# Between the two passes of a down projection: later pairs' preparation also waits its turn on ScalarE, and two sums between banks move behind the fourth pair

## The chip, the cores and the metric

The kernel runs on one core of one Trainium2 chip. The metric is device time in microseconds (us) of one execution. Before the change the median of three runs is 743.40 us (743.13 to 743.85).

## What is computed

One layer of a decoder trunk over 512 positions of width 1024, in float32:

```
h = RMSNorm(x);  q, k, v, gates = h @ W_in
m = sigmoid(gate_a) * (moba_attention @ W_a) + sigmoid(gate_b) * (stick_breaking_attention @ W_b)
x = x + m @ W_out
h = RMSNorm(x)
u_gate, u_val = split(causal_conv(h @ w_up))        # each 512 x 2816
x = x + (silu(u_gate) * u_val) @ w_down             # w_down: 2816 x 1024
out = RMSNorm_final(x)
```

Only the last product, the down projection `(silu(u_gate) * u_val) @ w_down`, is touched by the change.

## The kernel before, in words

**Every float32 product is three matmuls.** A matrix is split into a rounded part `hi` and a rest `lo`; `mm3` (lines 71 to 74) issues hi·hi, hi·lo and lo·hi on TensorE. The split of a weight tile of 128x1024 is one copy on ScalarE (`whi`, line 594) and one subtraction on VectorE (`wlo`, line 595), in `split_w`; that of an activation tile is the same pair of operations in `split_out` (lines 261 to 263).

**The down projection in two passes.** The 22 blocks of 128 rows of `w_down` are taken as nine pairs of blocks and four single ones (18 to 21). The pairs are multiplied as 2x2 block products by a scheme with seven instead of eight products. Eight PSUM banks hold the result, two for each quarter: `c11`, `c21`, `c12`, `c22` (each with `t` 0 and 1).

- The **first pass** (lines 603 to 616) adds four products for each pair: into c22, c21, c11 and c12. For the ninth pair the order is c11, c12, c21, c22.
- The **hand-over** (lines 637 to 649) combines the banks: `p1s` is a copy of c11 on ScalarE, `u2` = c12 + p1s, c21 is raised by u2, c12 becomes c22 + u2, and c22 becomes c21 + p5s, where `p5s` is a copy of the old c22 on ScalarE. The sums are on VectorE.
- The **second pass** (lines 650 to 654) adds three products for each pair: into c11, c21 and c12, 18 matmuls of 128x512. It does not touch c22.
- After the seventh pair 32 transposes (lines 667 to 670) add the residual to all eight banks, `x1R`; then come pairs eight and nine, then the four single blocks, `wl` (line 673), and the final norm.

**Preparation of a pair for the second pass** is `prep` (lines 628 to 634): VectorE makes `t2` (line 629), ScalarE and VectorE split the raw weight tile (`whi`, `wlo`), the activations (`xs`, three blocks of 256) and t2 (`w4`). That is three operations on ScalarE and four on VectorE. Two pairs are prepared ahead of the loop (line 636); the loop's turn j prepares pair j+2.

**What sets the order.** TensorE's program is in the order in which it is written. On the other engines a planner places instructions by its own estimate of when their inputs are there; each engine then works through its list in that fixed order. `tc.issue_after(x)` keeps the planner from placing what is inside ahead of instruction x on the engine of x. Before the change the preparation in the loop stands inside `tc.issue_after(last.ins)`, where `last` is an instruction of VectorE: the last sum of the hand-over, then the last operation of the pair before. Nothing of the kind holds it on ScalarE.

**Buffers.** Raw weight tiles have five buffers (`wraw`), split tiles seven (three in `wsp`, four in `dsp`), `xs` and `w4` three each. Loads are issued by SyncE (`rload`, line 586) in program order; the loads of `x1R` (line 661) and of `gb` (line 663) stand between those of the seventh and the eighth pair.

Of the kernel before, what the change touches and what calls it, by code (L numbers as in the profile page):

```python
# [10 lines left out]
F32 = mybir.dt.float32  # L11
F32R = mybir.dt.float32r
BF = mybir.dt.bfloat16
AF = mybir.ActivationFunctionType
# [13 lines left out]
NP = 9  # L28
# [10 lines left out]
def trunk_layer(ctx: ExitStack, tc: tile.TileContext, xT: bass.AP, w: bass.AP, vec: bass.AP,  # L39
                gfin: bass.AP, trig: bass.AP, out: bass.AP):  # L40
    nc = tc.nc

    def pool(stack, name, bufs, space=None, side=None):
        kw = {}
        if space is not None:
            kw["space"] = space
        if side is not None:
            kw["side"] = side
        return stack.enter_context(tc.tile_pool(name=name, bufs=bufs, reuse_waits="tile", **kw))
# [21 lines left out]
    def mm3(ps, a, b, start, stop, **kw):  # L71
        nc.tensor.matmul(ps, a[0], b[0], start=start, stop=False, **kw)  # L72
        nc.tensor.matmul(ps, a[0], b[1], start=False, stop=False, **kw)  # L73
        nc.tensor.matmul(ps, a[1], b[0], start=False, stop=stop, **kw)  # L74

    def blk(t, k, n=128):
        return t[0][:, k * n:(k + 1) * n], t[1][:, k * n:(k + 1) * n]
# [181 lines left out]
                fillers.pop(0)  # L259

    def split_out(hl, o):
        nc.scalar.activation(hl[:, 0], o, AF.Copy)
        return nc.vector.tensor_sub(hl[:, 1], o, hl[:, 0].bitcast(F32))

    stk = {}

    def rotate(g, n, i, ps, half):
        sc = (0.125, 1.0)[n]
        half[i] = [rt.tile([128, S], F32, name=f"r{i}{j}") for j in range(2)]
        for j in range(2):  # L270
            nc.vector.scalar_tensor_tensor(half[i][j], ps, sc, tg[:, j], op0=OP.mult, op1=OP.mult)
        if i:
            out = []
            for j, op in ((0, nc.vector.tensor_sub), (1, nc.vector.tensor_add)):
                o = half[0][j]
                op(o, o, half[1][1 - j])
                hl = mqkp.tile([128, 2, S], F32R, name=f"hl{j}")
                split_out(hl, o)
                out.append(hl)
            stk.setdefault(("a", g), []).append(out)  # L280
# [7 lines left out]
    def sb_qk(p):  # L288
        sc = {}

        def use(n, nm, ps):
            o = hlp.tile([128, S], F32, name="o")
            if nm == "q":
                nc.vector.scalar_tensor_tensor(o, ps, 0.125, rb, op0=OP.mult, op1=OP.mult)
            else:
                nc.vector.tensor_mul(o, ps, rb)
            sc[nm] = mqkp.tile([128, 2, S], F32R, name=f"hl{n}")
            split_out(sc[nm], o)

        for n, nm in enumerate(("q", "k")):  # L300
            yield from proj(("sqk", p, n), lambda ps: use(n, nm, ps))
        stk["b", p] = [(sc["q"], sc["k"], h * 64) for h in range(2)]
# [176 lines left out]
    for i in range(KT):  # L479
        if i >= NG:  # L480
            fillers.append(gates(i))
            fill(1000)
        wab = wload(("ab", i))
        g = pend[i]
        for b, br in enumerate("ab"):
            ps = pmm.tile([128, S], F32, name="mm")
            for p in range(4):
                mm3(ps, blk(wab, b * 4 + p), (yhl[br, p][:, 0], yhl[br, p][:, 1]), p == 0, p == 3)
            nc.vector.tensor_mul(g[b], g[b], ps)
        nc.vector.tensor_add(g[0], g[0], g[1])  # L490
        split_out(mhl[i], g[0])
# [48 lines left out]
    for i in range(FT):  # L540
        uc = []
        for b in range(2):
# [4 lines left out]
            t = up.tile([128, S], F32, name=f"t{b}")  # L547
# [11 lines left out]
        j = i // 2  # L559
# [17 lines left out]
    cq = {n: [pd.tile([128, 512], F32, name=f"{n}{t}") for t in range(2)] for n in ("c11", "c21", "c12", "c22")}  # L577
# [6 lines left out]
    def rload(key):  # L584
        raw = wraw.tile([128, 1024], F32, name="raw")
        nc.sync.dma_start(raw, w[WIDX[key]])
        return raw

    def split_w(raw):
        p = wsp if nsplit[0] % 7 < 3 else dsp  # L590
        nsplit[0] += 1
        hi = p.tile([128, 1024], F32R, name="whi")
        lo = p.tile([128, 1024], F32R, name="wlo")
        nc.scalar.activation(hi, raw, AF.Copy)  # L594
        nc.vector.tensor_sub(lo, raw, hi.bitcast(F32))  # L595
        return hi, lo

    def prod(bank, a, b, wt, h, start, stop, **kw):
        for t in range(2):
            sl = slice(t * 128, (t + 1) * 128)  # L600
            mm3(bank[t], (a[:, 0, b, sl], a[:, 1, b, sl]), blk(wt, h, 512), start, stop, **kw)
# [18 lines left out]
    cmb = pool(ctx, "cmb", 1)  # L620
# [7 lines left out]
    def prep(j, ra):  # L628
        nc.vector.tensor_sub(t2[j], ra[:, :512], t2[j])
        wa = split_w(ra)  # L630
        xs = xsp.tile([128, 2, 3, 256], F32R, name="xs")
        w4 = xsp.tile([128, 2, 512], F32R, name="w4")
        split_out(xs.rearrange("p a b c -> p a (b c)"), xb[j].rearrange("p b c -> p (b c)"))
        return xs, wa, (w4[:, 0], w4[:, 1]), split_out(w4, t2[j])

    ready = [prep(j, rload(("down", 2 * j + 1))) for j in range(2)]
    for t in range(2):
        p1s = cmb.tile([128, 512], F32, name=f"p1s{t}")
        nc.scalar.activation(p1s, cq["c11"][t], AF.Copy)
        u2 = cmb.tile([128, 512], F32, name=f"u2{t}")  # L640
        nc.vector.tensor_add(u2, cq["c12"][t], p1s)
        cq["u2", t] = u2
    for t in range(2):
        nc.vector.tensor_add(cq["c21"][t], cq["c21"][t], cq["u2", t])
    for t in range(2):
        p5s = cmb.tile([128, 512], F32, name=f"p5s{t}")
        nc.scalar.activation(p5s, cq["c22"][t], AF.Copy)
        nc.vector.tensor_add(cq["c12"][t], cq["c22"][t], cq["u2", t])
        last = nc.vector.tensor_add(cq["c22"][t], cq["c21"][t], p5s)
    for j in range(NP):  # L650
        xs, wa, w4, _ = ready.pop(0)
        prod(cq["c11"], xs, 0, wa, 0, False, False, skip_group_check=True)
        prod(cq["c21"], xs, 2, w4, 0, False, False, skip_group_check=True)
        prod(cq["c12"], xs, 1, wa, 1, False, False, skip_group_check=True)
        if j + 2 < NP:
            ra = rload(("down", 2 * j + 5))
            with tc.issue_after(last.ins):
                ready.append(prep(j + 2, ra))
                last = ready[-1][3]
        if j < KT // 2:  # L660
            nc.sync.dma_start(x1R[j], x1D[j])
        if j == KT // 2:
            nc.sync.dma_start(gb, gfin[None, :].to_broadcast([128, D]))
        if j == NP - 3:
            for t in range(QT):
                for h in range(2):
                    for i in range(4):
                        nc.tensor.matmul(acc[t, h][:, i * 128:(i + 1) * 128],  # L668
                                         x1R[2 * h + i // 2][:, i % 2, t * 128:(t + 1) * 128], ident,
                                         is_transpose=True, start=False, stop=False, skip_group_check=True)  # L670
# [3 lines left out]
    for t in range(QT):  # L674
        o = on[:, t]
# [91 lines left out]
```

## Time and profile before

| | us |
|---|---|
| median of three runs | 743.40 |
| the profiled execution's own time | 744.41 |
| its span, first to last instruction | 742.7 |
| TensorE busy with matmuls | 726.1 |
| VectorE busy | 511.2 |
| ScalarE busy | 327.0 |
| mean granted TensorE clock | 0.991 of full speed |

The time is that of the whole execution, the span that of the instructions in it. Busy time is summed over all instructions of an engine. Matmuls are pipelined and overlap in the records: two start 0.23 us apart, and each is shown with 0.39. An idle stretch of an engine is put down to what released it.

### The profile page before, as it was taken

What the parts mean: (1) busy time and instruction counts of PE and PEld (TensorE: products, weight loads), DVE (VectorE), ACT (ScalarE), POOL (GpSimd) and SP (SyncE); (2) the same over time, 40 slices, a digit from 0 to 9 for tenths busy, and PEclk for the clock granted to TensorE, in tenths of its full rate; (3) what the DMA queues carried; (4) which work ended last, traced back from release to release, by engine and by line L of the source; (5) the groups of instructions that cost most, each with busy time, mean ns of one, the idle gap of its engine ahead of it and who ended that gap; (6) DMA issues with size and microseconds to landing.
All of it is one profiled execution on the core that took longest, in us unless ns stands there. A gap on an engine that the chain in (4) does not pass through costs nothing.

```text
span 742.7 us, 9689 instructions
## 1 busy us (share of the span) xinstructions
PE 726.1 (98%) x3836; PEld 602.5 (81%) x3836; DVE 511.2 (69%) x724; ACT 327.0 (44%) x468; POOL 21.6 (3%) x40
## 2 busy tenths in 40 slices
PE   9999999999999999999999999999999999978996
PEld 6888888879788888888888888888888888856885
DVE  7778776692964544445648877878787888759813
ACT  7344453563652332334435434344443445465413
POOL 0000000320310000000000000000000000000000
PEclk9999999999999999999999999999999999997998
DMA  8432211121224323224432232332323134583203
GB/s 312 175 101 71 79 37 57 44 76 53 87 86 171 113 85 101 99 88 153 143 112 100 86 113 86 101 98 86 113 86 111 63 111 150 192 312 118 79 1 113
DMA packets 25389, 80.95 MB, mean 109 GB/s; under 512 B 2816, under 2 KB 3456, under 8 KB 25344
## 3 DMA queue, kind: packets, MB, share of 16 engines
q1 hardware_dynamic: 23472, 77.06, 30.9%
q10 hardware_dynamic: 1872, 3.28, 1.2%
q8 instruction: 30, 0.49, 0.3%
q14 instruction: 15, 0.12, 0.1%
HBM read 76.13 MB, written 4.19 MB: 108 GB/s over the span
## 4 chain that ended last, share of the span: by engine, by line
PE 70%; issue 20%; DVE 6%; DMA 3%; ACT 1%; POOL 0%; DVEq 0%; ACTq 0%; POOLq 0%
PE mm L72 20%; PE mm L74 19%; PE mm L73 19%; PE c L72 3%; DMA raw<-w 3%; PE c L73 3%; PE c L74 3%; DVE wlo L595 2%; PE tp L415 1%; PE tp L397 1%; ACT whi L594 1%; PE sc L330 1%; DVE raw L607 1%; DVE R L368 1%; PE c L668 0%
## 5 line engine op out<-in xcount | busy, mean ns | idle before, releaser
L67 ACT ACTIVATE whi<-raw 128x1024 fp32r<-128x1024 f32 (+2 forms) x106 | 107.0, 1013 | 212.8 <-PE mm L73 131.0
L72 PE MATMUL mm<-h,whi 128*128 128x512 f32 x352 | 137.1, 390 | 0.0
L74 PE MATMUL mm<-h,wlo 128*128 128x512 f32 x352 | 137.0, 389 | 0.0
L73 PE MATMUL mm<-h,whi 128*128 128x512 f32 x352 | 136.9, 389 | 0.0
L68 DVE TENSOR_TENSOR wlo<-raw,whi 128x1024 fp32r<-128x1024 f32 (+2 forms) x106 | 122.6, 1162 | 16.5 <-ACT whi L67 16.1
L72 PE MATMUL mm<-xg,whi 128*128 128x512 f32 x224 | 89.9, 401 | 0.0
L74 PE MATMUL mm<-xg,wlo 128*128 128x512 f32 x224 | 87.4, 390 | 0.0
L73 PE MATMUL mm<-xg,whi 128*128 128x512 f32 x224 | 87.3, 390 | 0.0
L73 PEld LDWEIGHTS mm<-h,whi 128*128 128x128 f32 x352 | 66.1, 188 | 13.8
L72 PEld LDWEIGHTS mm<-h,whi 128*128 128x128 f32 x352 | 66.1, 188 | 13.7
L74 PEld LDWEIGHTS mm<-h,wlo 128*128 128x128 f32 x352 | 66.1, 188 | 13.6
L546 DVE TENSOR_TENSOR u<-mm,rb 128x512 f32<-128x512 f32 x44 | 30.3, 690 | 30.6 <-PE mm L74 30.4
L72 PEld LDWEIGHTS mm<-xg,whi 128*128 128x128 f32 x224 | 42.1, 188 | 9.8 <-issue 1.4
L74 PEld LDWEIGHTS mm<-xg,wlo 128*128 128x128 f32 x224 | 42.0, 188 | 9.1
L73 PEld LDWEIGHTS mm<-xg,whi 128*128 128x128 f32 x224 | 42.2, 188 | 7.8
L594 ACT ACTIVATE whi<-raw 128x1024 fp32r<-128x1024 f32 x31 | 32.3, 1053 | 28.9 <-DVE raw L607 14.0
L595 DVE TENSOR_TENSOR wlo<-raw,whi 128x1024 fp32r<-128x1024 f32 x31 | 37.5, 1219 | 3.2 <-ACT whi L594 3.2
L548 ACT ACTIVATE t<-u,vecs 128x512 f32<-128x512 f32 x44 | 35.2, 802 | 2.0 <-DVE u L546 2.0
L439 DVE TENSOR_TENSOR g<-mm,rb 128x512 f32<-128x512 f32 x16 | 11.0, 687 | 34.4 <-PE mm L74 34.4
L551 DVE SCALAR_TENSOR_TENSOR t<-u,vecs,t 128x510 f32<-128x510 f32 x44 | 32.9, 749 | 1.3
L549 DVE SCALAR_TENSOR_TENSOR t<-u,vecs,t 128x511 f32<-128x511 f32 x44 | 32.8, 745 | 1.3 <-ACT t L548 1.3
L554 ACT ACTIVATE t<-t 128x512 f32<-128x512 f32 x22 | 13.8, 628 | 35.5 <-DVE t L551 35.5
(202 smaller groups left out, 1275.1 us busy)
## 6 DMA issues: line engine op xcount, KB each, us to landing
raw<-w SPq DMA_DIRECT2D x127, 512.0 KB, 3.3
xk<-xT SPq DMA_DIRECT2D x8, 256.5 KB, 5.1
x1T<-xT SPq DMA_DIRECT2D x8, 256.0 KB, 4.7
x1D<-x1T ACTq DMA_DIRECT2D x8, 256.0 KB, 2.0
x1R<-x1D SPq DMA_DIRECT2D x4, 512.0 KB, 7.8
raw<-w SPq DMA_DIRECT2D x6, 256.0 KB, 5.6
out<-on ACTq DMA_DIRECT2D x4, 256.0 KB, 2.5
out<-on SPq DMA_DIRECT2D x4, 256.0 KB, 2.7
```

Of the source, the lines that this page charges most:

```text
L67: nc.scalar.activation(hi[:, sl], raw[:, sl], AF.Copy)
L68: nc.vector.tensor_sub(lo[:, sl], raw[:, sl], hi[:, sl].bitcast(F32))
L72: nc.tensor.matmul(ps, a[0], b[0], start=start, stop=False, **kw)
L73: nc.tensor.matmul(ps, a[0], b[1], start=False, stop=False, **kw)
L74: nc.tensor.matmul(ps, a[1], b[0], start=False, stop=stop, **kw)
L546: nc.vector.tensor_mul(u, ps, rb2)
L548: nc.scalar.activation(t, u, AF.Identity, bias=cb[:, c:c + 1], scale=cw[:, 2, c:c + 1])
L549: nc.vector.scalar_tensor_tensor(t[:, 1:], u[:, :S - 1], cw[:, 1, c:c + 1], t[:, 1:], op0=OP.mult, op1=OP.add)
L551: nc.vector.scalar_tensor_tensor(t[:, 2:], u[:, :S - 2], cw[:, 0, c:c + 1], t[:, 2:], op0=OP.mult, op1=OP.add)
L554: nc.scalar.activation(uc[0], uc[0], AF.Silu)
L594: nc.scalar.activation(hi, raw, AF.Copy)
L595: nc.vector.tensor_sub(lo, raw, hi.bitcast(F32))
```

## The change

It makes four edits between the passes.

1. The copy `p5s` of the old c22 is gone. In its place stands `u3`, a copy of c21 on ScalarE, taken right after c21 was raised by u2. It is the same c21 that the sum into c22 read before.
2. The sums into c22 (c22 + u3 instead of c21 + p5s) move out of the hand-over into the loop's second turn, behind the preparation of the fourth pair.
3. `split_out` returns its ScalarE instruction too, and the preparation in the loop stands inside two `issue_after`: behind `last` on VectorE, and behind `lact` on ScalarE (at first the second copy `u3`, then the last ScalarE operation of the pair before).
4. In the text of the loop the preparation stands ahead of the three products, where it stood behind them.

```
     def split_out(hl, o):
-        nc.scalar.activation(hl[:, 0], o, AF.Copy)
-        return nc.vector.tensor_sub(hl[:, 1], o, hl[:, 0].bitcast(F32))
+        act = nc.scalar.activation(hl[:, 0], o, AF.Copy)
+        return act, nc.vector.tensor_sub(hl[:, 1], o, hl[:, 0].bitcast(F32))
...
     for t in range(2):
         nc.vector.tensor_add(cq["c21"][t], cq["c21"][t], cq["u2", t])
+        u3 = cq["u3", t] = cmb.tile([128, 512], F32, name=f"u3{t}")
+        lact = nc.scalar.activation(u3, cq["c21"][t], AF.Copy)
     for t in range(2):
-        p5s = cmb.tile([128, 512], F32, name=f"p5s{t}")
-        nc.scalar.activation(p5s, cq["c22"][t], AF.Copy)
-        nc.vector.tensor_add(cq["c12"][t], cq["c22"][t], cq["u2", t])
-        last = nc.vector.tensor_add(cq["c22"][t], cq["c21"][t], p5s)
+        last = nc.vector.tensor_add(cq["c12"][t], cq["c22"][t], cq["u2", t])
     for j in range(NP):
         xs, wa, w4, _ = ready.pop(0)
+        if j + 2 < NP:
+            ra = rload(("down", 2 * j + 5))
+            with tc.issue_after(last.ins), tc.issue_after(lact.ins):
+                ready.append(prep(j + 2, ra))
+                lact, last = ready[-1][3]
+        if j == 1:
+            for t in range(2):
+                with tc.issue_after(last.ins):
+                    last = nc.vector.tensor_add(cq["c22"][t], cq["c22"][t], cq["u3", t])
         prod(cq["c11"], xs, 0, wa, 0, False, False, skip_group_check=True)
         prod(cq["c21"], xs, 2, w4, 0, False, False, skip_group_check=True)
         prod(cq["c12"], xs, 1, wa, 1, False, False, skip_group_check=True)
-        if j + 2 < NP:
-            ra = rload(("down", 2 * j + 5))
-            with tc.issue_after(last.ins):
-                ready.append(prep(j + 2, ra))
-                last = ready[-1][3]
```

TensorE's list and SyncE's list of loads keep their order. ScalarE's list and VectorE's change in the rows below. Names carry a number for each buffer's use; c110 and c111 are the two banks of c11, c210 and c211 those of c21, and so on; xb0 to xb8 are the activations of the first to the ninth pair.

ScalarE at the hand-over, before: `whi_5699` and `whi_5712` belong to the first and second pair, the four after them to the third, fourth, fifth and seventh (raw_5886).

```order
L594 ACTIVATE whi_5699<-raw_5696 128x1024
L594 ACTIVATE whi_5712<-raw_5709 128x1024
L594 ACTIVATE whi_5761<-raw_5758 128x1024
L594 ACTIVATE whi_5793<-raw_5790 128x1024
L594 ACTIVATE whi_5825<-raw_5822 128x1024
L594 ACTIVATE whi_5889<-raw_5886 128x1024
L262 ACTIVATE xs_5703<-xb0_3581 128x768
L262 ACTIVATE w4_5704<-t20_3590 128x512
L262 ACTIVATE xs_5716<-xb1_3582 128x768
L262 ACTIVATE w4_5717<-t21_3591 128x512
L639 ACTIVATE p1s0_5722<-c110_5295 128x512
L639 ACTIVATE p1s1_5726<-c111_5296 128x512
```

The same place after the change:

```order
L594 ACTIVATE whi_5699<-raw_5696 128x1024
L594 ACTIVATE whi_5712<-raw_5709 128x1024
L262 ACTIVATE xs_5703<-xb0_3581 128x768
L262 ACTIVATE w4_5704<-t20_3590 128x512
L262 ACTIVATE xs_5716<-xb1_3582 128x768
L262 ACTIVATE w4_5717<-t21_3591 128x512
L639 ACTIVATE p1s0_5722<-c110_5295 128x512
L639 ACTIVATE p1s1_5726<-c111_5296 128x512
L646 ACTIVATE u30_5731<-c210_5297 128x512
L646 ACTIVATE u31_5734<-c211_5298 128x512
L594 ACTIVATE whi_5741<-raw_5738 128x1024
L262 ACTIVATE xs_5745<-xb2_3583 128x768
```

The four splits of later pairs went behind the copies of the hand-over, each to its own pair.

VectorE at the end of the hand-over, before (what stands ahead, `xs` and `w4` of the first two pairs and `u2`, is the same in both):

```order
L644 TENSOR_TENSOR c211_5298<-c211_5298,u21_5728 128x512
L648 TENSOR_TENSOR c121_5300<-c221_5302,u21_5728 128x512
L649 TENSOR_TENSOR c220_5301<-c210_5297,p5s0_5732 128x512
L649 TENSOR_TENSOR c221_5302<-c211_5298,p5s1_5736 128x512
L629 TENSOR_TENSOR t22_5306<-raw_5758,t22_5306 128x512
L595 TENSOR_TENSOR wlo_5762<-raw_5758,whi_5761 128x1024
L263 TENSOR_TENSOR xs_5765<-xb2_3583,xs_5765 128x768
L263 TENSOR_TENSOR w4_5766<-t22_5306,w4_5766 128x512
```

And after the change:

```order
L644 TENSOR_TENSOR c211_5298<-c211_5298,u21_5728 128x512
L648 TENSOR_TENSOR c121_5300<-c221_5302,u21_5728 128x512
L629 TENSOR_TENSOR t22_5306<-raw_5738,t22_5306 128x512
L595 TENSOR_TENSOR wlo_5742<-raw_5738,whi_5741 128x1024
L263 TENSOR_TENSOR xs_5745<-xb2_3583,xs_5745 128x768
L263 TENSOR_TENSOR w4_5746<-t22_5306,w4_5746 128x512
L629 TENSOR_TENSOR t23_5307<-raw_5770,t23_5307 128x512
L595 TENSOR_TENSOR wlo_5774<-raw_5770,whi_5773 128x1024
L263 TENSOR_TENSOR xs_5777<-xb3_3584,xs_5777 128x768
L263 TENSOR_TENSOR w4_5778<-t23_5307,w4_5778 128x512
L659 TENSOR_TENSOR c220_5301<-c220_5301,u30_5731 128x512
L659 TENSOR_TENSOR c221_5302<-c221_5302,u31_5734 128x512
```

The two sums into c22 went behind the preparation of the fourth pair.

ScalarE at the end of the preparations, after the change (raw_5900 and raw_5931 are the weights of the eighth and ninth pair, raw_6031 to raw_6049 those of the four single blocks):

```order
L594 ACTIVATE whi_5903<-raw_5900 128x1024
L594 ACTIVATE whi_6039<-raw_6037 128x1024
L262 ACTIVATE xs_5907<-xb7_3588 128x768
L262 ACTIVATE w4_5908<-t27_5311 128x512
L594 ACTIVATE whi_5934<-raw_5931 128x1024
L594 ACTIVATE whi_6033<-raw_6031 128x1024
L594 ACTIVATE whi_6045<-raw_6043 128x1024
L262 ACTIVATE xs_5938<-xb8_3589 128x768
L594 ACTIVATE whi_6051<-raw_6049 128x1024
L262 ACTIVATE w4_5939<-t28_5312 128x512
```

Here `w4_5939`, the ninth pair's, stands behind the splits of all four single blocks; before the change only three of them stood ahead of it.

## Rows read from the trace of the kernel before

**Rows 1.** The page: TensorE's granted clock in 40 equal slices of the span.

```profile
PEclk9999999999999999999999999999999999997998
```

**Rows 2.** Waits in the whole span: who waited for whom, us, times, longest us.

```profile
DVE xs L263 <- ACT xs L262: 8.0, 1, 8.0
...
PE c L72 <- ACT p1s L639: 5.5, 1, 5.5
...
PE c L72 <- DVE c L649: 2.1, 1, 2.1
```

**Rows 3.** Stretches: us, busy us of each engine, granted clock, DMA share, GB/s.

```profile
663.50:669.00 5.50, 0.03 (x2) 0.03 (x1) 2.30 (x3) 4.12 (x7) 0.00 (x0) 0.84 1.02 407
669.00:677.50 8.50, 6.42 (x14) 4.62 (x15) 8.50 (x14) 3.68 (x6) 0.00 (x0) 0.50 0.12 35
677.50:736.60 59.10, 59.08 (x277) 49.07 (x275) 32.24 (x53) 23.62 (x39) 0.00 (x0) 1.00 0.23 80
...
603.00:663.50 60.50, 60.50 (x267) 49.75 (x266) 47.33 (x51) 32.00 (x38) 0.00 (x0) 1.00 0.56 185
...
151.00:160.00 9.00, 8.18 (x46) 6.43 (x47) 8.59 (x12) 5.74 (x8) 2.55 (x4) 1.00 0.36 116
```

**Rows 4.** Chain that ended last, around the hand-over: start us, us, what.

```profile
655.19 3.50 DVE wlo L595 x3
658.71 6.07 DMA raw<-w
...
664.88 1.06 ACT whi L594
```

**Rows 5.** ScalarE in order of time: start us, us, what [idle before <-releaser].

```profile
652.79 2.94 ACT L594 ACTIVATE whi<-raw 128x1024 fp32r<-128x1024 f32 x3
...
664.88 1.06 ACT L594 ACTIVATE whi<-raw 128x1024 fp32r<-128x1024 f32 x1 [2.37 <-DMA raw<-w]
665.84 0.83 ACT L262 ACTIVATE xs<-xb 128x768 fp32r<-128x768 f32 x1
...
668.35 1.06 ACT L639 ACTIVATE p1s<-c 128x512 f32<-128x512 f32 x2
```

**Rows 6.** VectorE in order of time.

```profile
666.70 0.96 DVE L263 TENSOR_TENSOR xs<-xb,xs 128x768 fp32r<-128x768 f32 x1 [8.02 <-ACT xs L262]
...
670.85 0.69 DVE L644 TENSOR_TENSOR c<-c,u 128x512 f32<-128x512 f32 x1
...
672.04 0.69 DVE L644 TENSOR_TENSOR c<-c,u 128x512 f32<-128x512 f32 x1
...
673.24 1.28 DVE L649 TENSOR_TENSOR c<-c,p5s 128x512 f32<-128x512 f32 x2
674.43 0.68 DVE L629 TENSOR_TENSOR t<-raw,t 128x512 f32<-128x512 f32 x1
...
677.64 0.68 DVE L629 TENSOR_TENSOR t<-raw,t 128x512 f32<-128x512 f32 x1
```

**Rows 7.** TensorE in order of time, first pass's end and second pass's start.

```profile
654.73 0.39 PE L73 MATMUL c<-wlo,xa 128*128 128x512 f32 x1
...
663.12 0.39 PE L74 MATMUL c<-whi,xa 128*128 128x512 f32 x1
668.98 0.80 PE L72 MATMUL c<-whi,xs 128*128 128x512 f32 x1 [5.47 <-ACT p1s L639]
...
673.98 0.79 PE L72 MATMUL c<-w,xs 128*128 128x512 f32 x1 [2.08 <-DVE c L649]
...
679.84 0.39 PE L72 MATMUL c<-w,xs 128*128 128x512 f32 x1
```

**Rows 8.** Weight loads of line 586 between 640 and 705 us.

```profile
DMA to landing us min/median/max: 3.2/3.5/6.1
```

**Rows 9.** TensorE in order of time, a short wait in the attention.

```profile
151.82 0.88 PE L397 MATMUL tp<-ident,a 128*128 128x128 f32 x6 [1.01 <-ACT aT L400]
```

## Prediction

> **What bounds the kernel now.** I began with the page's granted clock. It is at nine or more tenths nearly everywhere; near the end one slice of 18.6 us stands at seven, and the last one, which holds the tail behind the last matmul, at eight [rows 1]. Then I read the waits of the whole span. TensorE waits 5.5 us once for `p1s` and 2.1 us once for a sum of line 649, and VectorE waits 8.0 us once for the first `xs` [rows 2]. All three lie at the hand-over between the passes. The stretches show what this does to TensorE: it is busy without a gap to 663.5, idle to 669, then it does only 14 matmuls in 8.5 us at a granted clock of 0.50 (that is 1.2 GHz), and from 677.5 on it is busy at 1.00 (2.4 GHz) to its end at 736.6 [rows 3]. So TensorE's work is the bound everywhere else, and the hand-over is a hole in it.
>
> Why does the hole exist? The chain of waits names a weight load of 6.07 us, issued when VectorE's three `wlo` were done, and the ScalarE split behind it [rows 4]. ScalarE's own list says the same: it splits three tiles to 655.73, goes on to four tiles of later pairs, and the last of these waits 2.37 us for its load until 664.88. Only then comes the first pair's `xs`, at 665.84 [rows 5]. Those four splits are no business of the hand-over: they belong to pairs three, four, five and seven. VectorE has had nothing to do for 8.02 us when `xs` releases it [rows 6], and TensorE's second pass has to wait for what VectorE and ScalarE do next.
>
> **The size of the hole.** In the first pass matmuls start every (663.12 − 654.73) / 37 = 0.2268 us. The last one starts at 663.12, and the 25th matmul of the second pass at 679.84, already at full pace [rows 7]. Without a hole it would start 25 × 0.2268 = 5.67 us after 663.12. It starts 16.72 us after it. **The hole costs 16.72 − 5.67 = 11.05 us**: 5.47 and 2.08 of waiting [rows 7], and about 3.5 of matmuls at half pace.
>
> **The change, part by part.** *Four splits leave ScalarE's way.* After 655.73 ScalarE goes straight to `xs` and `w4` of the first two pairs, which took 668.35 − 665.84 = 2.51 us [rows 5], so it is done with them at 658.2. c11's last matmul of the first pass is the 18th before the end: it starts at 663.12 − 18 × 0.2268 = 659.04 and is over at 659.4. The two `p1s` copies (1.06 us together [rows 5]) end by 660.1. They cost nothing on the path.
>
> *VectorE starts without its wait.* It is free when its three `wlo` end, at 658.69 [rows 4], and the first `xs` has been ready since 656.6. Its list to the end of the sums into c12 is unchanged and ran without a pause from 666.70 [rows 6]; it now runs 8.01 us earlier. The sum into c210 starts at 670.85 − 8.01 = 662.84 and ends at 663.5, that into c211 at 672.04 − 8.01 = 664.03 and ends at 664.7, and those into c12 end at 665.3. The banks that they read are ready: c21's last first-pass matmul starts at 661.76, c220's at 662.44.
>
> *The sums into c22 move.* Two sums (1.28 us [rows 6]) leave the hand-over, where TensorE waited 2.08 us for the first of them [rows 7]. They return once behind the fourth pair's preparation, covered by VectorE's lead there (below). TensorE does not touch c22 until the transposes behind the seventh pair.
>
> *`u3` takes the place of `p5s`*: two copies for two copies, but now in a chain, VectorE's sum, ScalarE's copy, TensorE's c21. The copy of c210 runs from about 663.6 to 664.2, that of c211 from about 664.8 to 665.4 (half of 1.06 us each, and up to 0.1 us from engine to engine: the first sum of line 649 ends near 673.9, and TensorE starts at 673.98 [rows 6, 7]). TensorE wants c110 at 663.35, c210 six matmuls on at 664.71, c211 at 665.39, c120 at 666.07. So the first bank has 0.5 us in hand, the second none, and c12 has 0.7. The bounds of this new wait are 0 (the copy is quick) and 0.5 us (both hops and a restart: 0.80 against 0.39 us of a first matmul [rows 7]). I take 0.15, near the lower end, since the sum on the clock comes out at about zero.
>
> *Preparations in turn.* TensorE takes 18 × 0.2268 = 4.08 us for a pair, so pair three is due at 671.5 and each later one 4.08 us on. VectorE takes 677.64 − 674.43 = 3.21 us for a preparation [rows 6]. For pair three it starts at 665.2, waits about 0.9 us for the split that now comes in turn on ScalarE, and ends at 669.3: 2.2 us in hand. Pair four ends at 672.5 (due 675.6), and with the 1.28 us of sums pair five at 677.0 (due 679.7). Each further pair gains 0.87 us. If ScalarE's split of 1.06 us never overlapped anything, a preparation would take 4.27 us, 0.19 more than TensorE needs, and six of them would lose 1.1 us of the 2.2. So this costs nothing, from 0 up to a bound of 0.5 with a poor start.
>
> *Loads.* SyncE's order is the same. The loads of pairs three to seven wait for `wlo` operations that do not move; those of pair eight on wait for VectorE's later ones, which come earlier with the rest. A load lands after 3.2 to 6.1 us [rows 8]. All preparations, four splits of single blocks included, end by about 695; the ninth pair is due at 696 even without the transposes ahead of it, and its `w4` a product later.
>
> *Sum.* 11.05 − 0.15 = **10.9 us less**. The profiled execution took 744.41 us; that gives 733.5. It stood 1.0 above the median of the runs, so the median becomes 743.4 − 10.9 = **732.5 us**. What bounds then is TensorE's list from first to last, with the old tail of 6.1 us.
>
> **The clock, weighed.** Rows: 1.00 before the hole, 0.84 in the idle stretch, 0.50 behind it, 1.00 again after 8.5 us of matmuls with one wait [rows 3]; a wait of 1.01 us in the attention [rows 9] leaves the clock at 1.00 [rows 3]. I conclude that the half pace belongs to the idle time and goes with it. If it came from the second pass itself, some 3.5 us would stay and the gain be 7.4. The Trainium skill (TensorE: Matmul & The Clock Gate, Part 1) calls throttling the default that activity lifts. By that rule of the Trainium skill the sum would be the 10.9, not the 7.4; the trace agrees, with its 0.50 behind the idle stretch alone.
>
> **Rivals.** *The new chain leaks* (8 in 100). TensorE waits 1 to 3 us in all, for `u3` or for pair three, because VectorE, ScalarE and TensorE now follow one another with no time in hand. For it: c211 has none. Against it: each link is a row of before. It gives 733.4 to 735.5; if such a wait also halved the pace once, 3.5 more. The trace has no gap between 2.08 and 5.47 us, and none but the 1.01 before which the clock was full, so it cannot say which side this one would fall on. The Trainium skill (TensorE: Matmul & The Clock Gate, "Why this matters for your kernels") warns of idle gaps between bursts of matmuls for this reason.
>
> *A hidden wait in front of the first `xs`* (4 in 100). Its buffers lie where the first pass's activations were. Before, ScalarE came to them only after the first pass, so a wait for TensorE would not have shown. If `xs` can't start before 663.5, the list from 665.84 moves up by only 2.3 us, and with 1.2 us of sums gone the gain is 3.5: 739.9. Against it: only the oldest pairs' buffers lie there, whose matmuls are long over.
>
> *The change does not do what it says* (1 in 100): the load of 6.07 us still ends the hole through some other instruction, and the time stays at 743.4.
>
> *Slower* (2 in 100). On ScalarE the ninth pair's `w4` now stands behind the splits of all four single blocks, and `xs` behind three of them. Each needs a load and a buffer that TensorE frees late (the last one behind the sixth pair, at 687.8). If these waits pile up, TensorE stops in front of pair nine. Up to 696 this costs nothing; beyond it each us costs one, and from 707 on the kernel is slower than before: at 709 it is 732.5 + 13 = 745.5. A load would have to take over 15 us; the longest took 6.1 [rows 8].
>
> *Forecast* (85 in 100): 732.5, by itself 731.6 to 733.4, from the bounds 0 and 1.0 of the two small waits and the spread of the runs shown.
>
> **How the numbers follow.** The range takes the forecast's own span and nearly all of the leaking chain: 731.5 to 735.0. It leaves out the hidden wait, no effect, slower, and a little of the others. 0.2% is 1.5 us, about what a measurement can tell from no change. Faster by more: forecast, leak and hidden wait, 0.97; within: 0.01; slower: 0.02.
>
> **What the profile would show.** Right: no wait of TensorE over 0.5 us at the hand-over, a clock of 1.00 through 660 to 700, ScalarE's first `xs` near 655.7, VectorE's first `xs` near 658.7, transposes about 11 us earlier. The forecast is wrong if TensorE waits for `u3`, if the clock falls to 0.50 without an idle stretch, if `xs` still starts behind 663, or if TensorE waits for a preparation in any later pair.

## The result, and the profile after

| | before | after |
|---|---|---|
| median | 743.60 us (743.13 to 743.85, 4 runs) | **733.98 us** (733.46 to 734.47, 4 runs) |
| ratio of the two, 95% interval | | 0.9871, 0.9854 to 0.9888 |
| the profiled execution's own time | 744.41 | 733.46 |
| its span | 742.7 | 731.7 |
| TensorE busy with matmuls in it | 726.1 | 722.1 |
| mean granted TensorE clock | 0.991 | 0.999 |

The change makes the kernel faster by 9.6 us by the medians (8.3 to 10.9 by the interval), and by 10.95 us from the one profiled execution to the other. Forecast were 732.5 us and 10.9 us. The 743.60 is the median of four executions, one more than stood behind the 743.40 on which the forecast was built.

The page after, its granted clock in 40 slices, which answers to [rows 1]:

```profile
PEclk9999999999999999999999999999999999999999
```

The slice at seven is gone. All waits of TensorE in the span after (the two waits at the hand-over in [rows 2] are no longer there):

```profile
PE tp L397 <- ACT aT L400: 1.7, 2, 1.0
PE mm L149 <- DVE warmb L87: 1.2, 1, 1.2
PE q L187 <- ACT whi L67: 0.5, 1, 0.5
```

The two stretches behind the last matmul of the first pass, after (busy us of PE, weight loads, DVE, ACT and POOL, then granted clock, share of the DMA engines, GB/s). In [rows 3] TensorE was idle here, and then at 0.50:

```profile
663.00:669.00 6.00, 6.00 (x28) 4.83 (x27) 5.58 (x9) 4.91 (x7) 0.00 (x0) 1.00 1.02 412
669.00:674.00 5.00, 5.00 (x24) 4.14 (x23) 5.00 (x8) 2.60 (x4) 0.00 (x0) 1.00 0.70 264
```

ScalarE's own list after, which answers to [rows 5] (start, duration, instruction, idle time before it and what ended that):

```profile
653.23 2.94 ACT L594 ACTIVATE whi<-raw 128x1024 fp32r<-128x1024 f32 x3
656.08 0.83 ACT L262 ACTIVATE xs<-xb 128x768 fp32r<-128x768 f32 x1
...
658.81 1.28 ACT L639 ACTIVATE p1s<-c 128x512 f32<-128x512 f32 x2
663.49 0.60 ACT L646 ACTIVATE u<-c 128x512 f32<-128x512 f32 x1 [3.41 <-DVE c L644]
664.69 0.60 ACT L646 ACTIVATE u<-c 128x512 f32<-128x512 f32 x1 [0.60 <-DVE c L644]
665.18 1.05 ACT L594 ACTIVATE whi<-raw 128x1024 fp32r<-128x1024 f32 x1
```

The first `xs` follows the third split at once, at 656.08 instead of 665.84. The next split, that of pair three, comes behind the second `u3`.

VectorE's list after, which answers to [rows 6]:

```profile
655.23 3.49 DVE L595 TENSOR_TENSOR wlo<-raw,whi 128x1024 fp32r<-128x1024 f32 x3
658.63 0.95 DVE L263 TENSOR_TENSOR xs<-xb,xs 128x768 fp32r<-128x768 f32 x1
...
662.77 0.69 DVE L644 TENSOR_TENSOR c<-c,u 128x512 f32<-128x512 f32 x1
...
663.97 0.69 DVE L644 TENSOR_TENSOR c<-c,u 128x512 f32<-128x512 f32 x1
...
665.16 0.68 DVE L629 TENSOR_TENSOR t<-raw,t 128x512 f32<-128x512 f32 x1
666.27 1.23 DVE L595 TENSOR_TENSOR wlo<-raw,whi 128x1024 fp32r<-128x1024 f32 x1 [0.42 <-ACT whi L594]
...
668.28 0.69 DVE L263 TENSOR_TENSOR w<-t,w 128x512 fp32r<-128x512 f32 x1
...
672.09 1.29 DVE L659 TENSOR_TENSOR c<-c,u 128x512 f32<-128x512 f32 x2
...
693.27 0.69 DVE L263 TENSOR_TENSOR w<-t,w 128x512 fp32r<-128x512 f32 x1
```

It goes from `wlo` to `xs` without a pause; the 8.02 us are gone. Of the new order on ScalarE it feels 0.42 us, at 666.27, where `wlo` waits for pair three's split.

TensorE's list after, which answers to [rows 7]. 663.14 is the last matmul of the first pass, 665.41 and 665.68 are the first and second into c211, 668.89 is the 25th of the second pass, and 692.02 the first of the residual's transposes, which stood at 702.97 before:

```profile
663.14 0.39 PE L74 MATMUL c<-whi,xa 128*128 128x512 f32 x1
663.37 0.39 PE L72 MATMUL c<-whi,xs 128*128 128x512 f32 x1
...
665.41 0.43 PE L72 MATMUL c<-w,xs 128*128 128x512 f32 x1
665.68 0.39 PE L73 MATMUL c<-w,xs 128*128 128x512 f32 x1
...
668.89 0.39 PE L72 MATMUL c<-w,xs 128*128 128x512 f32 x1
...
692.02 3.66 PE L671 MATMUL c<-ident,x1R 128*128 128x128 f32 x32
```

By the prediction's own measure the hole after is 668.89 − 663.14 − 5.67 = 0.08 us, where it was 11.05. The difference, 10.97, is the 10.95 by which the profiled times differ.

### The profile page after: what moved, and what is told of

The parts are those of the page before. It is cut to its first block, busy times and chain, and to the rows that moved or that the text cites. A ratio compares the mean times of both kernels' runs of the same rounds, so it can differ in the third digit from the quotient of the medians.

```text
span 731.7 us, 9687 instructions
## 1 busy us (share of the span) xinstructions
PE 722.1 (99%) x3836; PEld 600.4 (82%) x3836; DVE 511.0 (70%) x724; ACT 326.5 (45%) x468; POOL 21.7 (3%) x40
## 4 chain that ended last, share of the span: by engine, by line
PE 78%; issue 19%; DVE 1%; ACT 0%; POOL 0%; POOLq 0%; DVEq 0%; ACTq 0%
PE mm L72 20%; PE mm L73 20%; PE mm L74 20%; PE c L72 5%; PE c L74 5%; PE c L73 5%; PE tp L415 1%; PE tp L397 1%; PE sc L330 1%; DVE R L368 1%; PE c L671 0%; DVE a L370 0%; DVE wlo L68 0%; PE tp L117 0%; DVE on L701 0%
```

## The experiments

Theory A, mine, says that in the kernel before ScalarE stands in a split of a later pair, which waits for a load or a buffer, and that everything behind it, half pace included, follows from that. The rivals: the sums moved out of the hand-over bring the gain (B); the half pace belongs to the second pass and not to the idle time (C); the load's lateness, not the place of the split, is what was cured (D).

### The turn on ScalarE alone

The changed kernel with its edits 1 and 2 undone: `p5s` and the sums into c22 are back in the hand-over.

```
         nc.vector.tensor_add(cq["c21"][t], cq["c21"][t], cq["u2", t])
-        u3 = cq["u3", t] = cmb.tile([128, 512], F32, name=f"u3{t}")
-        lact = nc.scalar.activation(u3, cq["c21"][t], AF.Copy)
     for t in range(2):
-        last = nc.vector.tensor_add(cq["c12"][t], cq["c22"][t], cq["u2", t])
+        p5s = cmb.tile([128, 512], F32, name=f"p5s{t}")
+        lact = nc.scalar.activation(p5s, cq["c22"][t], AF.Copy)
+        nc.vector.tensor_add(cq["c12"][t], cq["c22"][t], cq["u2", t])
+        last = nc.vector.tensor_add(cq["c22"][t], cq["c21"][t], p5s)
...
-        if j == 1:
-            for t in range(2):
-                with tc.issue_after(last.ins):
-                    last = nc.vector.tensor_add(cq["c22"][t], cq["c22"][t], cq["u3", t])
```

> Edit 3 alone: later pairs' preparation waits its turn on ScalarE (behind the copies p5s), while the two sums into c22 stay in the hand-over as before. Theory (four splits of later pairs stood in ScalarE's list ahead of the first xs; a short wait does not lower the clock): the 8 us wait of VectorE is gone, and TensorE waits only for the first of the two sums, which ends at 665.9 where c21 is wanted at 664.7: a wait of 1.2 us at a granted clock of 1.00, so 1.2 above the changed kernel, 735.2. Rival 1 (the sums in the hand-over, which TensorE waited for by name, are the larger part): most of the hole stays, 739 to 742. Rival 2 (any wait here lowers the clock): 1.2 + 3.5 above the changed kernel, 738.7.

Measured: 735.21 us (734.70 to 735.77), against 744.47 before on that chip: ratio 0.9875, 0.9863 to 0.9888. TensorE's only wait at the hand-over with the 25th matmul of the second pass, and the stretch around the wait:

```profile
666.15 0.50 PE L72 MATMUL c<-w,xs 128*128 128x512 f32 x1 [1.18 <-DVE c L649]
...
670.39 0.39 PE L72 MATMUL c<-w,xs 128*128 128x512 f32 x1
```

```profile
663.00:669.00 6.00, 4.82 (x21) 3.67 (x20) 5.40 (x8) 4.43 (x6) 0.00 (x0) 1.00 0.95 384
```

The turn on ScalarE alone brings 9.3 us. What is left is a wait of 1.18 us for the sum of line 649, at a clock that stays at 1.00. By the prediction's measure the hole is 670.39 − 663.22 − 5.67 = 1.50 us (663.22 is the last matmul of the first pass): the wait, and 0.3 more around the matmul that starts after it. Moving the sums takes away 1.50 − 0.08 = 1.4 us of that by the profiles, and 735.21 − 733.98 = 1.2 us by the medians, which come from two sets of runs. (Edit 4 does nothing by itself: with the preparation back behind the products in the text, every engine has the same instructions in the same order.)

### The moved sums alone

The changed kernel without the turn on ScalarE:

```
-            with tc.issue_after(last.ins), tc.issue_after(lact.ins):
+            with tc.issue_after(last.ins):
```

> Edits 1 and 2 alone: u3 takes the place of p5s and the sums into c22 move behind the fourth pair, but nothing holds later preparations on ScalarE, and seven splits stand ahead of the first xs again. Theory: the wait for the load until about 664.9 stays, TensorE starts its second pass near 669.0 at half clock, and only the 2.1 us wait for the sums shrinks, to about 0.4 to 0.7 (the copy u3 of c210 ends near 672.2, c11's six matmuls near 671.5). Gain 1.4 to 1.7: 741.9 to 742.3. Rival 1 (the sums are the larger part): 735 to 738.

Measured: 742.02 us (740.16 to 743.05), ratio 0.9965, 0.9953 to 0.9977. ScalarE and TensorE there:

```profile
664.41 1.06 ACT L594 ACTIVATE whi<-raw 128x1024 fp32r<-128x1024 f32 x1 [2.39 <-DMA raw<-w]
665.37 0.83 ACT L262 ACTIVATE xs<-xb 128x768 fp32r<-128x768 f32 x1
```

```profile
668.50 0.79 PE L72 MATMUL c<-whi,xs 128*128 128x512 f32 x1 [5.12 <-ACT p1s L639]
...
671.74 0.80 PE L72 MATMUL c<-w,xs 128*128 128x512 f32 x1 [0.32 <-ACT u L646]
```

The wait of 2.1 has become 0.32, and the wait of 5 us with the half pace behind it stays: the seventh split still stands in front of `xs`. Theory B falls. The time lies in the forecast, but the gain does not: 744.47 − 742.02 = 2.4 us (1.7 to 3.5 by the interval) where 1.4 to 1.7 were expected; before stood higher on this chip than the 743.6 from which the forecast was reckoned. By the medians the two parts don't add: 9.3 and 2.4 alone, 9.6 together. The waits say why: without the turn the sums' wait falls from 2.08 to 0.32, behind it there is only the one of 1.18 left to remove.

### Only the seventh pair waits its turn

The kernel before, with one preparation, that of the seventh pair, held on ScalarE behind the copies:

```
-        nc.scalar.activation(p5s, cq["c22"][t], AF.Copy)
+        lact = nc.scalar.activation(p5s, cq["c22"][t], AF.Copy)
...
-            with tc.issue_after(last.ins):
+            with ExitStack() as turn:
+                turn.enter_context(tc.issue_after(last.ins))
+                if j + 2 == 6:
+                    turn.enter_context(tc.issue_after(lact.ins))
```

> The kernel before, but only the seventh pair's preparation waits its turn on ScalarE (behind p5s): the one split whose load landed last goes, the three of pairs three to five stay ahead of the first xs. Theory: ScalarE comes to the first xs when the fifth pair's split ends, near 662.5 instead of 665.84. Everything to TensorE's first matmul moves 3.3 us up: the gap of 5.5 becomes 2.2, and the one of 2.1 for the sums stays. The gain is 3.3, 740.3, if the clock falls as before, and up to 6.8, 736.8, if gaps of 2.2 and 2.1 leave it at 1.00. Rival (the load itself is the bound and its landing frees something else): no change, 743.6.

Measured: 741.18 us (739.12 to 742.68), ratio 0.9952, 0.9938 to 0.9967. Now the split of the fifth pair is the last in the way:

```profile
661.96 1.06 ACT L594 ACTIVATE whi<-raw 128x1024 fp32r<-128x1024 f32 x1 [1.86 <-DMA raw<-w]
662.93 0.83 ACT L262 ACTIVATE xs<-xb 128x768 fp32r<-128x768 f32 x1
```

```profile
666.06 0.50 PE L72 MATMUL c<-whi,xs 128*128 128x512 f32 x1 [2.41 <-ACT p1s L639]
...
667.33 0.39 PE L74 MATMUL c<-whi,xs 128*128 128x512 f32 x1
671.07 0.80 PE L72 MATMUL c<-w,xs 128*128 128x512 f32 x1 [3.35 <-DVE c L649]
671.66 0.63 PE L73 MATMUL c<-w,xs 128*128 128x512 f32 x1
```

`xs` follows the last split, whichever pair it belongs to. The gain is the lower one forecast, 744.47 − 741.18 = 3.3 us. The 740.3 was 0.9 us too good because the 3.3, read in the execution of 744.41, had been taken off the median of 743.6; 744.41 − 3.3 is 741.1. How the gain came about was not foreseen: the clock did not fall behind the first gap, so TensorE came through c11 at full pace, reached the sums earlier, and its second wait grew from 2.08 to 3.35 us, with the half pace behind that one. Time gained ahead of the sums came back as a wait in front of them.

### The kernel before, unchanged, twice more

> The kernel before, unchanged, for a second profile. The profiled hole of 11.05 us is more than the 9.6 between the medians. Theory A: the hole's size varies from execution to execution with the landing of one load in a busy stretch (6.07 us in the profile shown), and the profiled execution, 0.8 above its median, had a large one: here the load lands sooner, the hole is 9.5 to 10.5, and the span is shorter by as much. Theory B: the hole is 11.0 again, and the missing 1.4 lies elsewhere, in the changed kernel.

> The kernel before for a third profile. Theory A: the hole again differs from the 11.05 and the one of the second profile by how late ScalarE's last of seven splits starts (664.88 and 662.84 there), and the span follows it. Theory B: the hole is the same as in one of them and the span differs elsewhere.

Measured: 742.36 us in one execution and 744.24 in the other. The last of the seven splits and TensorE's wait in the first:

```profile
662.84 1.06 ACT L594 ACTIVATE whi<-raw 128x1024 fp32r<-128x1024 f32 x1 [1.89 <-PE c L74]
```

```profile
666.93 0.80 PE L72 MATMUL c<-whi,xs 128*128 128x512 f32 x1 [3.42 <-ACT p1s L639]
...
671.94 0.51 PE L72 MATMUL c<-w,xs 128*128 128x512 f32 x1 [2.08 <-DVE c L649]
...
673.45 0.63 PE L72 MATMUL c<-whi,xs 128*128 128x512 f32 x1
...
677.76 0.39 PE L72 MATMUL c<-w,xs 128*128 128x512 f32 x1
```

and in the second:

```profile
664.83 1.06 ACT L594 ACTIVATE whi<-raw 128x1024 fp32r<-128x1024 f32 x1 [1.48 <-DMA raw<-w]
```

```profile
668.92 0.80 PE L72 MATMUL c<-whi,xs 128*128 128x512 f32 x1 [5.29 <-ACT p1s L639]
```

The kernel before has a hole of another size in each of the three profiled executions, and the time follows it: 744.41 − 5.47, 742.36 − 3.42 and 744.24 − 5.29 are 738.94, 738.94 and 738.95. In the first of these two the whole hole is 677.76 − 663.13 − 5.67 = 8.96 us by the prediction's measure, less than the 9.5 to 10.5 that were expected. What releases the split varies too: in the first of these two executions it is TensorE, in the second and in [rows 5] the load. So it isn't one late load (D): the hole ends with the last split in ScalarE's way, whether that waits for its load or for TensorE.

Nor did the change make the load earlier. SyncE issues the same load at 658.7 in the changed kernel's profile too, where it landed 5.7 us later:

```profile
L586 SPq DMA_DIRECT2D raw<-w x1: 328/328/328, 658.7 to 658.7; - x1
...
DMA to landing us min/median/max: 5.7/5.7/5.7
```

That is 664.4, against 664.8 before [rows 4]. The load is about as late as it was; the first `xs`, at 656.08, no longer stands behind it.

### A gap of chosen size in the changed kernel

Four, and in a second kernel seven, more operations on VectorE ahead of the sums of the hand-over; each writes a tile's larger value of itself and itself, so no value changes. TensorE then waits for `u3` at the place where the changed kernel has no wait.

```
+    late = ready[-1][3][1]
+    for _ in range(4):
+        with tc.issue_after(late.ins):
+            late = nc.vector.tensor_tensor(t2[0], t2[0], t2[0], op=OP.max)
...
-        nc.vector.tensor_add(u2, cq["c12"][t], p1s)
+        with tc.issue_after(late.ins):
+            nc.vector.tensor_add(u2, cq["c12"][t], p1s)
```

> The changed kernel with four extra operations of VectorE (each a maximum of a tile with itself, 128x512, so no value changes) ahead of the hand-over's sums. They take 4 x 0.60 us and move the sums, the copies u3 and with them TensorE's c21 later; c11's six matmuls run as before. This makes one gap of TensorE of a size that the trace before did not have. Theory (a gap under some size costs itself alone): a gap of 2.4 us with the granted clock at 1.00 throughout, 734.0 + 2.4 = 736.4. Rival (any such gap lowers the clock): 3.5 more, 739.9.

> The same with seven extra operations: a gap of 4.2 us. Theory (the clock falls in a gap of this size, as it did in the gap of 3.4 us of the second profile of the kernel before): 734.0 + 4.2 and up to 3.5 for matmuls at half pace, 740 to 741.7, with a granted clock of 0.50 behind the gap. Rival (the gap itself is all): 738.2 with the clock at 1.00.

Measured: with four, 735.93 us (735.10 to 738.35; ratio to before 0.9888, 0.9867 to 0.9910); with seven, 739.89 us (739.17 to 740.27; ratio 0.9933, 0.9916 to 0.9949). With four:

```profile
666.89 0.50 PE L72 MATMUL c<-w,xs 128*128 128x512 f32 x1 [2.04 <-ACT u L651]
667.22 0.40 PE L73 MATMUL c<-w,xs 128*128 128x512 f32 x1
```

```profile
663.00:669.00 6.00, 3.73 (x16) 2.46 (x15) 5.55 (x9) 2.16 (x4) 0.00 (x0) 1.00 1.02 415
```

With seven:

```profile
669.17 0.80 PE L72 MATMUL c<-w,xs 128*128 128x512 f32 x1 [4.08 <-ACT u L651]
669.77 0.63 PE L73 MATMUL c<-w,xs 128*128 128x512 f32 x1
...
675.66 0.39 PE L72 MATMUL c<-w,xs 128*128 128x512 f32 x1
```

```profile
663.00:669.00 6.00, 2.09 (x10) 1.39 (x8) 5.83 (x11) 0.47 (x1) 0.00 (x0) 0.86 1.02 415
669.00:674.00 5.00, 4.83 (x11) 3.73 (x12) 4.58 (x8) 3.86 (x6) 0.00 (x0) 0.50 0.24 79
```

The same matmuls at the same place run at 1.00 behind a gap of 2.04 us and at 0.50 (1.2 GHz) behind one of 4.08. Theory C falls: at this place the half pace follows the idle time and not the second pass (one fall without a wait in front of it is told in the last section). The gaps came out a little shorter than the 2.4 and 4.2 that were expected, and 739.89 lies just below the 740 to 741.7. By the prediction's measure the hole with seven is 675.66 − 663.34 − 5.67 = 6.65 us (663.34 is the last matmul of the first pass): 4.1 is the gap, and 2.6 what the slower start and the slower matmuls behind it cost. With four, one of the four runs stood at 738.35, with a mean clock of 0.995 against 0.998 to 0.999 in the others. It was not profiled; that the clock fell there is likely and not shown.

### The changed kernel, unchanged, once more

> The changed kernel, unchanged, for a second profile. Theory A (the missing 1.3 us between the sum of the prediction and the medians lies in the kernel before, whose hole varies from execution to execution, and the changed kernel has no hole to vary): no wait of TensorE over 0.5 us at the hand-over, a clock of 1.00 there, span 731.5 to 732.7. Theory B (the changed kernel has a hole of its own in some executions): a wait of 0.5 to 1.5 us at the hand-over or behind a preparation.

Measured: 733.98 us, and again no wait of TensorE at the hand-over. It is 0.52 slower than the first profile, and TensorE's part in that is there long before the hand-over. In the attention, the products of its weights with the values (line 415) in this execution, and the same ones in the first profile of the changed kernel:

```profile
224.07 4.59 PE L415 MATMUL tp<-aT,vb 128*64 128x128 f32 x80
```

```profile
223.46 4.59 PE L415 MATMUL tp<-aT,vb 128*64 128x128 f32 x80
```

It is 0.61 us late there already, more than the whole difference. So the difference between these two executions doesn't come from the hand-over; the other executions of the changed kernel were not profiled.

## Why the prediction was right, and where it was off

**The hole.** 11.05 us were to vanish but for 0.15. 10.97 vanished. The two experiments with one part of the change each bear out both causes: the splits in ScalarE's way (9.3 by itself) and the sums (1.2 to 1.4 behind it).

**ScalarE and VectorE start early.** Forecast 655.7 for ScalarE's first `xs`, found 656.08; forecast 658.69 for VectorE's, found 658.63. The sums into c210 and c211 were put at 662.84 and 664.03 and stood at 662.77 and 663.97. That VectorE's list moves up as a whole, by the length of its one wait, held to a tenth.

**The new wait for `u3`.** Bounds 0 and 0.5, taken 0.15. The first matmul into c211 stands 0.27 in front of the second, 0.04 more than the usual step; the whole second pass up to its 25th matmul loses 0.08. The copy of c211 ended at 665.29, 0.12 before TensorE used it. It could not have been much later. The experiment with four operations shows what a later one costs.

**Preparations in turn.** Pair three ended at 668.97 (forecast 669.3), pair four at 672.18 (672.5), and the last, that of the ninth pair, at 693.96, with the splits of the single blocks done ahead of it (about 695 for all). The wait for pair three's split was 0.42 and not 0.9; the difference is in TensorE's favour and moved nothing. The sums into c22 ran at 672.09, covered as said.

**The clock.** 1.00 through the whole hand-over, as the forecast had it: the sum of 10.9 and not 7.4. The Trainium skill (TensorE: Matmul & The Clock Gate, "Why this matters for your kernels") warns of idle gaps between bursts of matmuls; the runs agree, with 0.50 behind the gaps of 3.35 us and more, and with 1.00 behind the three of 1.18 to 2.41 us.

**The rivals.** No leak, no hidden wait in front of `xs`, no pile-up in front of pair nine.

**What was off** is the last step of the sum, from the profiled execution to the median: "It stood 1.0 above the median of the runs, so the median becomes 743.4 − 10.9". That takes the 1.0 to stay. But the execution profiled before stood above its median because its hole was a large one: the wait behind `p1s` was 5.47 us there, and 3.42 us in the execution of 742.36. The hole went, and the 1.0 with it. Without that step the forecast is 744.41 − 10.9 = 733.5, and the profiled execution took 733.46. The other half of a microsecond is the changed kernel's own spread, 733.46 to 734.47. So the measured 733.98 lies in the range of 731.5 to 735.0, but above the 731.6 to 733.4 that was given for the forecast by itself. The room above 733.4 had been left for a leaking chain, and no chain leaked: the account of the hand-over was right, that the range held was in part luck.

Nothing in these runs points to a faster version of the hand-over: TensorE has no gap left in it.

## What to carry to other kernels

An engine that works through a fixed list can be held by an instruction that nobody needs yet, as ScalarE was here by a split of the seventh pair: where TensorE waits, read the list of the engine that it waits for upward, to the first instruction that waits for a load or a buffer, and move that one behind the urgent work. A term of the sum that varies between executions must be subtracted from the execution in which it was measured, not from the median. A copy or a sum that TensorE doesn't need at a hand-over can be paid for later, in the first place where its engine has a lead.

## What the runs showed of the hardware that I had not expected

TensorE came to each of these gaps at full pace. Behind 1.18, 2.04 and 2.41 us the next matmuls started full (0.50, then 0.39 or 0.40 each), behind 3.35, 3.42, 4.08, 5.12, 5.29 and 5.47 at half pace (0.79 or 0.80, then 0.63). In the prediction's words the trace had no gap between 2.08 and 5.47; these fill it, except between 2.41 and 3.35.

A gap's own size does not tell everything. The second gap of the kernel before, 2.08 us behind six matmuls at half pace, was the same in three executions. In two of them the matmuls behind it went on at half pace (0.79 in [rows 7], 0.80 in the execution of 744.24). In the execution of 742.36 they ran full from 671.94 and fell to 0.63 again at 673.45, with no wait in front of them. The granted clock, last but two in this row, had already risen in the gap itself, with TensorE idle:

```profile
669.90:671.90 2.00, 0.00 (x0) 0.00 (x0) 2.00 (x5) 0.12 (x1) 0.00 (x0) 0.99 0.01 4
```

What raised the clock there, and what ended the full pace, isn't settled.
